# Preparing summed weight operands in two in-place series on SP's queue, with six own places for the sample states

## The chip, the cores and the metric

One core of one Trainium2 chip runs the whole program. The metric is device time in microseconds (us) of one execution. The engines are TensorE (PE, with its weight loads PEld), VectorE (DVE), ScalarE (ACT), GpSimd (POOL) and SyncE (SP). SP computes nothing here; it issues DMAs, in the order in which they stand in its stream, and where one has to wait, all behind it wait. The same holds for the DMAs that ACT issues between its own instructions.

## The reference

One inference step of two layers on a prompt of 2048 tokens and on 64 sample tokens (8 sequences of 8). Layer 0 is a gated DeltaNet, layer 1 a RetNet with 4 heads. The change lies in layer 1:

```
p = rmsnorm(x, norm_w) @ w_in           # x (L, 1024), w_in (1024, 6144)
q, k, v, gate = split(p)                # 4 heads: q,k 256 wide, v and gate 512 wide
q, k = rotary(q), rotary(k) / 16
o, S = retention(q, k, v, S0)           # S_t = gamma_h S_{t-1} + k_t^T v_t ; o_t = q_t S_t
o = rmsnorm(o, onorm) * silu(gate)
y = x + o @ w_out
```

The sample tokens start from given states (8 sequences x 4 heads x 256 x 512), which are read, used, updated and written back: 16 pieces of 128 x 512 in each head.

## The kernel before, in words

The prompt is cut into 4 blocks of 512 tokens (n = 0 to 3). Layer 0 runs over all blocks first, then layer 1; in both, four heads or groups follow one another in a block. Every matrix product in float32 is made of three products in a reduced format: each operand is split into a high part (a cast on ACT) and the rest (a subtraction on DVE). `wload` (L192) loads a weight tile into one of two places `wraw`, casts it on ACT (L196) and subtracts on DVE (L197).

Layer 1 computes the projections of block 0 in the plain way, with the 64 sample tokens beside them (width 576). Blocks 1 to 3 use a scheme with 7 products of half-size operands in place of 8 (`quad`, `vquad`, `seven`). It needs sums and differences of the quarters of each weight matrix, A21+A22 and so on, already split in two parts. They are prepared once, during block 0, and kept in DRAM (`wh_d`): 4 heads x 6 weight tiles x 4 combinations. That is the generator `prep_head` (L1022), four tasks in a chain. For each of the 24 weight tiles it loads two 128x1024 halves (`Rw`, tag "ta", 2 places), makes four sums of 128x512 on POOL (`Sm`, L1032 to L1035), splits each on ACT and DVE into `Wo` (tag "tc", 2 places), and stores it with 512 KB. All these loads and stores are issued by ACT.

The order comes from two levels. A small planner (`_Pipe`) advances a clock with each matmul it emits and lets side tasks (the retention `ret_prompt`, `ret_sample`, `prep_head`) emit their next piece when their time has come; a `yield 2.5` says that the next piece is due 2.5 us later by this clock. A tile scheduler then sets the final order of each engine's stream. Each engine runs its stream strictly in order.

At head 3 of block 0, `pipe.wait(ptask)` (L1524) emits all that is left of the preparation, and then `build_halves` (L1066) makes the halves of the activations for block 1. Its operands T2, T3 and N4 lie in the same places "ta", "tb" and "tc" that the preparation used. No projection of block 1 can start before.

`ret_sample` (L1226) runs once per head, for the 16 state pieces: a ring of five places, two in the tile "st" and three in the ring `xst`, which the output projection (`outproj_B`, L1322, tile `xr`) uses too. In groups of four pieces, PE multiplies the queries with the four states (`os`), then makes four updates (`ps`), DVE combines each with its state (L1303), SP stores it and loads the next piece into the place that came free (L1270).

Of the kernel before, what the change touches and what calls it, by code (L numbers as in the profile page):

```python
# [10 lines left out]
F32 = mybir.dt.float32  # L11
# [80 lines left out]
def tile_hybrid(ctx: ExitStack, tc: tile.TileContext, a: dict, S: int):  # L92
# [926 lines left out]
            return q[0][0], q[1][0], q[0][1], q[1][1]  # L1019
        return [src[j][:, 512 * i : 512 * i + 512] for j in range(2) for i in range(2)]  # L1020

    def prep_head(h):  # L1022
        pb = B.pb
        for t, (src, vkind) in enumerate(quads(h)):
            R = [pb.tile([128, 1024], F32, tag="ta", bufs=2, name="Rw") for _ in range(2)]
            for j in range(2):
                ACT.dma_start(R[j], src[j])
            A11, A12, A21, A22 = quarters(R, vkind)
            Sm = [pb.tile([128, 512], F32, tag="tb", bufs=4, name="Sm") for _ in range(4)]
            sm = [v3(x, 256) if vkind else x for x in Sm]  # L1030
            yield 5.0
            PL.tensor_tensor(sm[0], A21, A22, op=ALU.add)  # L1032
            PL.tensor_tensor(sm[1], sm[0], A11, op=ALU.subtract)
            PL.tensor_tensor(sm[2], A11, A21, op=ALU.subtract)
            PL.tensor_tensor(sm[3], A12, sm[1], op=ALU.subtract)  # L1035
            for i, x in enumerate(Sm):
                o = pb.tile([128, 2, 512], F32R, tag="tc", bufs=2, name="Wo")
                yield 1.5
                split(o[:, 0], o[:, 1], x)
                yield 2.5  # L1040
                ACT.dma_start(wh_d[h][4 * t + i], o.rearrange("p t c -> p (t c)").bitcast(F32))

    def wstream(h):

# [21 lines left out]
    def build_halves(n, rb):  # L1066
        pb = B.pb
        xs_, ts = [None] * 8, [None] * 8
        xn = [None] * 8
        for p in range(4):  # L1070
            xp = [sb.tile([128, 2, 2, XC], F32R, tag=f"xn{p}", name=f"xn{p}")]
            for j in range(2):
                xn[2 * p + j] = xp[0][:, j]
        T2, N4 = ([pb.tile([128, 2, 2, 256], F32R, tag=t, bufs=2, name=t) for _ in range(2)] for t in ("ta", "tc"))
        T3 = [pb.tile([128, 2, 256], F32R, tag="tb", bufs=4, name="tb") for _ in range(4)]
        T2, N4 = ([t[kt // 2][:, kt % 2] for kt in range(4)] for t in (T2, N4))
        l, r = slice(0, 256), slice(256, 512)
        for kt in range(4):
            xs, t = [], []
            for k in (kt, kt + 4):  # L1080
                x = xst("xs")
                nc.sync.dma_start(x[:, :TB], x1_d[k * 128 : (k + 1) * 128, n * TB : (n + 1) * TB])
                y = sb.tile([128, XC], F32, tag="tmp", bufs=2, name="xt")
                V.scalar_tensor_tensor(y[:, :TB], x[:, :TB], nw[:, 1, k : k + 1], rb[:, :TB],
                                       op0=ALU.mult, op1=ALU.mult)
                xs.append(x)
                t.append(y)
            lo_, hi_ = xn[kt], xn[kt + 4]
# [14 lines left out]

# [122 lines left out]
    def ret_sample(h, QRs, KRs, vraw, GTs, OG):  # L1226
# [16 lines left out]
        for half in range(2):  # L1243
            for k in range(2):
# [10 lines left out]
        ACT.activation(K3, v3(kT, 256), AF.Copy, scale=kd)  # L1255
        V.scalar_tensor_tensor(K3[64:128], v3(kT, 256)[64:128], kd[64:128], K3[64:128].bitcast(F32),
                               op0=ALU.mult, op1=ALU.subtract)
        loads, st2 = [], []

        def load(i):  # L1260
            if i >= 16:
                return
            if i % 5 < 2:
                if i % 5 == 0:
                    st2.append(pb.tile([128, 2, 512], F32, tag="st", name="st"))
                st = st2[-1][:, i % 5]
            else:
                st = xst("st")[:, :512]
            b, k = 4 * (i // 8) + i % 4, i // 4 % 2
            nc.sync.dma_start(st, a["state_ret"][b, h, k * 128 : (k + 1) * 128, :])  # L1270
            loads.append(st)

        for i in range(5):
            load(i)
        yield 6.0
        for half in range(2):
            o = po("os")
            mm(o, Ash[:, half * 128 : (half + 1) * 128], V3[:, half], start=True, stop=False)
            for k in range(2):
                yield LAT_ST  # L1280
                i0 = 8 * half + 4 * k
                t = pipe.t

                def query(b4):
                    r = slice(32 * b4, 32 * b4 + 32)
                    return mm(o[r], QRs[:, k, half * 128 + 32 * b4 : half * 128 + 32 * b4 + 32], loads[i0 + b4],
                              start=False, stop=(k == 1))

                last_in = query(3)
                with tc.issue_after(last_in.ins):  # L1290
                    for b4 in range(3):
                        query(b4)
                pipe.t = t + 1.0
                for b4 in range(4):
                    i = i0 + b4
                    st = loads[i]
                    Kt = pb.tile([128, 128], F32R, tag=("Kt", "Qc")[b4 % 2], name="Kts")
                    ACT.activation(Kt, K3[:, half, k * 128 : (k + 1) * 128].bitcast(F32), AF.Copy,
                                   scale=B.kms[:, h, b4 : b4 + 1])
                    yield 0.8  # L1300
                    p = pc("ps") if b4 % 2 == 0 else pf("ps")
                    mm(p, Kt, V3[:, half])
                    V.scalar_tensor_tensor(st, st, g8, p, op0=ALU.mult, op1=ALU.add)  # L1303
                    nc.sync.dma_start(a["ret_s"][4 * half + b4, h, k * 128 : (k + 1) * 128, :], st)
                    if i:
                        load(i + 4)
            yield from until(posts[-1])
            on = ret_on(o, h, 2)

# [97 lines left out]
    for n in range(NB):  # L1407
        for h in range(4):
# [66 lines left out]
            if start:  # L1475
# [1 line left out]
                pb = B.pb  # L1477
                Gs, GTs = GTs, pb.tile([128, 4, NS], F32, tag="GTs", bufs=2, name="GTs")
                V.tensor_copy(GTs, Gs)
                for j in range(BH):  # L1480
                    ptask = pipe.add(prep_head(j), 9, [ptask])
            if h == 3 and n + 1 < NB:
                rb = ret_rb(n + 1)
            pipe.wait(lastret)
# [36 lines left out]
                vraw = pb.tile([128, 512], F32, tag="p2", name="vraw")[:64]  # L1521
                ACT.copy(vraw, pvs[:64])
            if h == 3 and n + 1 < NB:
                pipe.wait(ptask)  # L1524
                xo = build_halves(n + 1, rb)
            end = n == NB - 1 and h == 3
            if pendB and not end:
# [141 lines left out]
```

## Time and profile before

| | us |
|---|---|
| median of 3 runs (3439.61 to 3457.56) | 3439.98 |
| the profiled execution | 3458.83 |
| its span | 3455.9 |
| layer 1, block 0, from the first prepared tile to the last value matmuls of head 3 | 1515 to 2027 |
| from there until the output projection of head 2 runs on | 2027 to 2085 |
| blocks 1 to 3 | 2100 to 3456 |

The profiled execution took 18.9 us longer than the median. PE is busy in 93% of the span. Rows say for an instruction when it starts, how long it takes, and in square brackets how long its engine had been idle and what ended that wait. TensorE's clock has two levels, 1.2 and 2.4 GHz; PEclk 0.92 means that the granted clock was on average 0.92 of the higher one.

### The profile page before, as it was taken

What the parts mean: (1) busy time and instruction counts of PE and PEld (TensorE: products, weight loads), DVE (VectorE), ACT (ScalarE), POOL (GpSimd) and SP (SyncE); (2) the same over time, 40 slices, a digit from 0 to 9 for tenths busy, and PEclk for the clock granted to TensorE, in tenths of its full rate; (3) what the DMA queues carried; (4) which work ended last, traced back from release to release, by engine and by line L of the source; (5) the groups of instructions that cost most, each with busy time, mean ns of one, the idle gap of its engine ahead of it and who ended that gap; (6) DMA issues with size and microseconds to landing.
All of it is one profiled execution on the core that took longest, in us unless ns stands there. A gap on an engine that the chain in (4) does not pass through costs nothing. (4 is left out here: it accounts for less than half of the span.)

```text
span 3455.9 us, 59249 instructions
## 1 busy us (share of the span) xinstructions
PE 3228.3 (93%) x21436; PEld 2820.6 (82%) x21436; DVE 2400.7 (69%) x5406; ACT 1582.9 (46%) x3655; POOL 494.5 (14%) x714
## 2 busy tenths in 40 slices
PE   7999999999999999998898868999999999999997
PEld 6999777778688788877777747889988899889896
DVE  6876888787868878556574666566676666776666
ACT  6555564455435555324242443344443344533443
POOL 1211011001010000012322230111101111111110
PEclk9999999999999999999999989999999999999999
DMA  4333544435443243456878777887677867778675
GB/s 131 96 95 100 176 126 132 132 102 157 120 138 109 88 135 83 142 190 229 293 250 289 246 247 230 271 276 252 228 253 251 279 242 244 235 270 286 216 246 171
DMA packets 371413, 669.79 MB, mean 194 GB/s; under 512 B 119456, under 2 KB 169392, under 8 KB 371120
## 3 DMA queue, kind: packets, MB, share of 16 engines
q1 hardware_dynamic: 350384, 590.49, 53.1%
q10 hardware_dynamic: 20736, 75.51, 6.0%
q8 instruction: 169, 2.77, 0.3%
q14 instruction: 124, 1.02, 0.1%
HBM read 517.08 MB, written 146.68 MB: 192 GB/s over the span
## 5 line engine op out<-in xcount | busy, mean ns | idle before, releaser
L101 PE MATMUL pp<-xn,w 128*128 128x288 f32 (+1 forms) x5456 | 1107.2, 351 | 21.8 <-DVE xr L1336 5.5
L101 PEld LDWEIGHTS pp<-xn,w 128*128 128x128 f32 x5456 | 861.6, 192 | 131.8 <-issue 18.5
L101 PE MATMUL pp<-OG,w 128*128 128x512 f32 (+1 forms) x2880 | 597.2, 366 | 27.4 <-DVE xr L1336 18.1
L101 PEld LDWEIGHTS pp<-OG,w 128*128 128x128 f32 x2880 | 491.8, 195 | 114.2 <-DVE xr L1336 18.0
L197 DVE TENSOR_TENSOR w<-wraw,w 128x1024 fp32r<-128x1024 f32 x272 | 347.4, 1278 | 97.3 <-ACT w L196 92.8
L196 ACT CAST w<-wraw 128x1024 fp32r<-128x1024 f32 x272 | 286.1, 1052 | 250.3 <-PE pp L101 126.8
L101 PE MATMUL sq<-xn,w 128*128 128x256 f32 x2304 | 310.6, 284 | 7.5 <-DVE GT L1106 3.5
L101 PEld LDWEIGHTS sq<-xn,w 128*128 128x128 f32 x2304 | 287.9, 188 | 15.1 <-issue 5.4
L210 ACT CAST w<-wraw 128x512 fp32r<-128x512 f32 x216 | 129.5, 623 | 218.5 <-PE pp L101 75.2
L1336 DVE TENSOR_TENSOR xr<-xr,pp 128x512 f32<-128x512 f32 (+1 forms) x160 | 92.4, 592 | 143.2 <-PE pp L101 105.9
L211 DVE TENSOR_TENSOR w<-wraw,w 128x512 fp32r<-128x512 f32 x216 | 147.9, 698 | 60.2 <-ACT w L210 56.7
L743 DVE SCALAR_TENSOR_TENSOR acc<-pp,cw,acc 128x511 f32<-128x511 f32 (+2 forms) x216 | 160.4, 743 | 20.6 <-ACT acc L740 20.2
L101 PE MATMUL sv<-w,xn 128*128 128x256 f32 x1152 | 147.1, 285 | 6.6 <-DMA w<-wh_d 5.1
L101 PEld LDWEIGHTS sv<-w,xn 128*128 128x128 f32 x1152 | 142.1, 192 | 8.9 <-DVE KR L1004 3.2
L101 PE MATMUL o<-Sc,Qc 128*128 128x512 f32 x360 | 100.9, 404 | 11.0 <-DVE Sc L211 5.9
L488 DVE TENSOR_TENSOR VP<-VP,tm 128x66 f32<-128x66 f32 (+26 forms) x510 | 107.0, 210 | 4.4
L486 DVE TENSOR_TENSOR tm<-LP,VP 128x66 f32<-128x66 f32 (+26 forms) x510 | 104.9, 206 | 6.1 <-DMA LP<-sl 2.1
L101 PE MATMUL p<-Vh,Kt 128*128 128x512 f32 x384 | 107.8, 412 | 0.0
L101 PE MATMUL pv<-w,xn 128*128 128x512 f32 x384 | 101.8, 413 | 4.0 <-ACT w L196 1.9
L210 ACT CAST Wo<-Sm 128x512 fp32r<-128x512 f32 x96 | 58.7, 617 | 96.1 <-DMA wh_d<-Wo 69.9
L210 ACT CAST OG<-og 128x256 fp32r<-128x256 f32 x192 | 71.6, 405 | 66.4 <-DVE og L1215 33.1
L1151 POOL TENSOR_TENSOR so<-oss,rsc 128x1 f32<-128x1 f32 x72 | 15.5, 215 | 580.8 <-ACT on L1149 580.8
(434 smaller groups left out, 5727.1 us busy)
## 6 DMA issues: line engine op xcount, KB each, us to landing
w<-wh_d SPq DMA_DIRECT2D x288, 512.0 KB, 5.4
wraw<-in_w_in_a SPq DMA_DIRECT2D x128, 512.0 KB, 3.7
wh_d<-Wo ACTq DMA_DIRECT2D x96, 512.0 KB, 4.6
x_d<-xr SPq DMA_DIRECT2D x160, 256.0 KB, 3.9
wraw<-in_w_qkg SPq DMA_DIRECT2D x144, 256.0 KB, 4.3
xr<-x_d SPq DMA_DIRECT2D x128, 256.0 KB, 4.5
wraw<-in_w_out_b SPq DMA_DIRECT2D x64, 512.0 KB, 4.2
wraw<-in_w_v SPq DMA_DIRECT2D x72, 256.0 KB, 5.1
```

Of the source, the lines that this page charges most:

```text
L101: ins = nc.tensor.matmul(out, lhsT, rhs, start=start, stop=stop)
L196: ACT.copy(w[:, 0, :], raw)
L197: V.tensor_tensor(w[:, 1, :], raw, w[:, 0, :].bitcast(F32), op=ALU.subtract)
L210: ACT.copy(hi, x)
L211: V.tensor_tensor(lo, x, hi.bitcast(F32), op=ALU.subtract)
L486: V.tensor_tensor(tv, LP[:, m, m + 1 : m + 1 + n].unsqueeze(2).to_broadcast([128, n, ncol]), VP[:, m, 0:ncol].unsqueeze(1).to_broadcast([1 ...
L488: V.tensor_tensor(VP[:, m + 1 : m + 1 + n, 0:ncol], VP[:, m + 1 : m + 1 + n, 0:ncol], tv, op=ALU.subtract)
L743: V.scalar_tensor_tensor(acc[:, sh:], ap[:, : TB - sh], cw[:, ct, j : j + 1], acc[:, sh:], op0=ALU.mult, op1=ALU.add)
L1151: PL.tensor_tensor(so, ss, B.rsc[:, h, col : col + 1], op=ALU.add)
L1336: V.tensor_tensor(xs[:, s:e], xs[:, s:e], p[:, : e - s], op=ALU.add)
```

## The change

The preparation becomes two tasks without a chain, `prep(0)` and `prep(1)`. Each handles one half (256 of 512 columns of every quarter, index `u`) of all 24 weight tiles. A step loads four quarters of 128x256 with four DMAs, makes the four sums with four POOL instructions of 128x256, casts all four in one ACT instruction of 128x1024 back into the tile that was loaded, subtracts in one DVE instruction in place in the sums, and stores the two parts with two DMAs of 512 KB in runs of 256 columns. The first series uses the two places of "ta", the second those of "tb" (now as large as "ta"). All six DMAs of a step are issued by SP. So each step needs both places of its series, and the next load goes into the place that the cast's result is stored from.

The 16 state pieces of a head use six places of their own ("st" with two, the freed "tc" with four) in heads 0 to 2; `xst` is then left to the output projection. Head 3, where "tc" holds N4, keeps five.

```
+    def halves_of(src, vkind, u):
+        if vkind:
+            return [src[j][:, 512 * u + 256 * i : 512 * u + 256 * i + 256] for i in range(2) for j in range(2)]
+        return [src[j][:, 512 * i + 256 * u : 512 * i + 256 * u + 256] for j in range(2) for i in range(2)]
...
-    def prep_head(h):
+    def prep(u):
         pb = B.pb
-        for t, (src, vkind) in enumerate(quads(h)):
-            R = [pb.tile([128, 1024], F32, tag="ta", bufs=2, name="Rw") for _ in range(2)]
-            for j in range(2):
-                ACT.dma_start(R[j], src[j])
-            A11, A12, A21, A22 = quarters(R, vkind)
-            Sm = [pb.tile([128, 512], F32, tag="tb", bufs=4, name="Sm") for _ in range(4)]
-            yield 5.0
-            PL.tensor_tensor(sm[0], A21, A22, op=ALU.add)
...
-            for i, x in enumerate(Sm):
-                o = pb.tile([128, 2, 512], F32R, tag="tc", bufs=2, name="Wo")
-                yield 1.5
-                split(o[:, 0], o[:, 1], x)
-                yield 2.5
-                ACT.dma_start(wh_d[h][4 * t + i], o.rearrange("p t c -> p (t c)").bitcast(F32))
+        tag = ("ta", "tb")[u]
+        for h, t in ((h, t) for h in range(BH) for t in range(6)):
+            src, vkind = quads(h)[t]
+            R = pb.tile([128, 4, 256], F32R, tag=tag, bufs=2, name="Rw")
+            Sm = pb.tile([128, 4, 256], F32, tag=tag, bufs=2, name="Sm")
+            A11, A12, A21, A22 = (R[:, i, :].bitcast(F32) for i in range(4))
+            for x, y in zip((A11, A12, A21, A22), halves_of(src, vkind, u)):
+                nc.sync.dma_start(x, y)
+            yield 6.0
+            PL.tensor_tensor(Sm[:, 0], A21, A22, op=ALU.add)
...
+            yield 4.5
+            ACT.copy(R, Sm)
+            V.tensor_tensor(Sm.bitcast(F32R), Sm, R.bitcast(F32), op=ALU.subtract)
+            yield 3.0
+            out = wh_d[h][4 * t : 4 * t + 4].rearrange("x p (l v c) -> p x l v c", l=2, v=2)[:, :, :, u, :]
+            nc.sync.dma_start(out[:, :, 0], R.bitcast(F32))
+            nc.sync.dma_start(out[:, :, 1], Sm)
+            yield 4.5
...
+        ring = 5 if h == 3 else 6
...
-            if i % 5 < 2:
-                if i % 5 == 0:
-                    st2.append(pb.tile([128, 2, 512], F32, tag="st", name="st"))
-                st = st2[-1][:, i % 5]
+            j = i % ring
+            if j < 2 or h < 3:
+                if j % 2 == 0:
+                    tag, bufs = ("st", 1) if j < 2 else ("tc", 2)
+                    st2[0] = pb.tile([128, 2, 512], F32, tag=tag, bufs=bufs, name="st")
+                st = st2[0][:, j % 2]
...
                     if i:
-                        load(i + 4)
+                        load(i + ring - 1)
...
-                for j in range(BH):
-                    ptask = pipe.add(prep_head(j), 9, [ptask])
+                ptask = [pipe.add(prep(u), 9, lat=9.0 * u) for u in range(2)]
...
-                pipe.wait(ptask)
+                pipe.wait(*ptask)
```

How the streams move is shown at three places. The numbers in the names tell buffers apart. The first is ACT's stream before, right behind the copies of head 3's values (`Vt`, `vraw`); `Wo<-Sm` is one cast of the preparation, `wh_d3` its place in DRAM.

```order
L210 CAST Wo_21820<-Sm_21812 128x512
L210 CAST Wo_21824<-Sm_21813 128x512
L1027 DMA Rw_21837<-in_w_v 128x1024
L1041 DMA wh_d3_76<-Wo_21820 128x1024
L1041 DMA wh_d3_76<-Wo_21824 128x1024
L196 CAST w_22072<-wraw_22071 128x1024
L210 CAST Wo_21828<-Sm_21814 128x512
L196 CAST w_22143<-wraw_22142 128x1024
L210 CAST Wo_21832<-Sm_21815 128x512
L1041 DMA wh_d3_76<-Wo_21828 128x1024
L1027 DMA Rw_21864<-in_w_v 128x1024
```

The changed stream, five short instructions behind the same copies; `Rw<-Sm` is one cast of a step, of twice the columns.

```order
L1045 CAST Rw_21737<-Sm_21738 128x1024
L1045 CAST Rw_21743<-Sm_21744 128x1024
L196 CAST w_21984<-wraw_21983 128x1024
L196 CAST w_22055<-wraw_22054 128x1024
L1045 CAST Rw_21765<-Sm_21766 128x1024
L1045 CAST Rw_21771<-Sm_21772 128x1024
L196 CAST w_22126<-wraw_22125 128x1024
L1045 CAST Rw_21793<-Sm_21794 128x1024
L210 CAST Sc_22408<-Sr_21521 128x512
L1045 CAST Rw_21799<-Sm_21800 128x1024
L1045 CAST Rw_21821<-Sm_21822 128x1024
L1045 CAST Rw_21827<-Sm_21828 128x1024
```

Before, 12 casts in all stand behind the last `Vt` copy, which is 3 of the 24 weight tiles, with ACT's own DMAs among them; now 10 casts (8 of them shown, 2 further on), which is 5 of the 24, and no DMA. The streams of the retention (`Sc`, and further on `Ah`) stand behind them.

SP's changed stream at the same place, for the last two steps of both series; `Rw<-in_w_v` are loads, `wh_d3<-Rw` and `wh_d3<-Sm` the stores of the two parts, the others tables.

```order
L1038 DMA Rw_21821<-in_w_v 128x256 x4
L1038 DMA Rw_21827<-in_w_v 128x256 x4
L1177 DMA rmk_22299<-in_rmask 128x128
L1473 DMA cs_22796<-in_rope 128x2x512
L1049 DMA wh_d3_76<-Rw_21821 128x4x256
L1050 DMA wh_d3_76<-Sm_21822 128x4x256
L1049 DMA wh_d3_76<-Rw_21827 128x4x256
L1050 DMA wh_d3_76<-Sm_21828 128x4x256
L1038 DMA Rw_21849<-in_w_v 128x256 x4
L1038 DMA Rw_21855<-in_w_v 128x256 x4
```

None of these loads and stores stood on SP before. The eight loads of a pair of steps stand behind all four stores of the pair before.

PE's stream before, at the states of the third head in block 0, from the last update `ps` of the third group of states to the queries `os` of the fourth; `pp<-xn` is projection work that fills the time.

```order
L101 MATMUL ps<-V_20757,Kts 128x512
L101 MATMUL pp<-xn_16129,w 128x288
L101 MATMUL pp<-xn_16144,w 128x288 x12
L101 MATMUL pp<-xn_16159,w 128x288 x12
L101 MATMUL pp<-xn_16114,w 128x288 x12
L101 MATMUL pp<-xn_16129,w 128x288 x12
L101 MATMUL pp<-xn_16144,w 128x288
L101 MATMUL os<-st,QRs 32x512 x4
```

The same place in the changed stream, from a little earlier.

```order
L101 MATMUL pp<-xn_16144,w 128x288 x3
L101 MATMUL ps<-V_20863,Kts 128x512
L101 MATMUL pp<-xn_16159,w 128x288 x4
L101 MATMUL ps<-V_20863,Kts 128x512
L101 MATMUL pp<-xn_16159,w 128x288 x8
L101 MATMUL os<-st,QRs 32x512 x4
```

The queries of the fourth group moved forward: 8 matmuls lie between the last update and them, where there were 50.

## Rows read from the trace of the kernel before

**Rows 1.** The head of the page.
```profile
span 3455.9 us, 59249 instructions
```

**Rows 2.** Stretches: us, busy us of each engine (instructions), PEclk, DMA share, GB/s.
```profile
1515.00:2027.00 512.00, 445.91 (x2521) 373.96 (x2520) 318.55 (x552) 203.66 (x423) 143.85 (x128) 0.92 0.76 263
2027.00:2085.00 58.00, 26.86 (x102) 18.19 (x101) 39.02 (x71) 26.87 (x57) 14.09 (x14) 0.67 0.55 192
...
2700.00:2800.00 100.00, 99.02 (x694) 91.74 (x693) 63.27 (x112) 39.67 (x82) 11.58 (x17) 1.00 0.74 251
```

**Rows 3.** Timeline of PE at the end of block 0: start, us, instruction, idle before.
```profile
2026.82 4.95 PE L101 MATMUL pp<-OG,w 128*128 128x288 f32 x36
...
2048.87 0.80 PE L101 MATMUL o<-Vh,Ah 128*128 128x512 f32 x1 [15.34 <-ACT Vh L210]
...
2085.14 5.17 PE L101 MATMUL pp<-OG,w 128*128 128x288 f32 x20 [1.67 <-DVE xr L1336]
```

**Rows 4.** Waits from 1515 to 2085 us: total, times, longest.
```profile
ACT Wo L210 <- DMA wh_d<-Wo: 69.9, 27, 5.3
...
PE os L101 <- DMA st<-in_state_ret: 31.0, 10, 6.9
...
DVE xr L1336 <- DMA xr<-x_d: 18.1, 8, 5.9
PE pp L101 <- DVE xr L1336: 17.0, 8, 5.5
...
ACT w L196 <- DMA xr<-x_d: 8.2, 1, 8.2
...
PE pv L101 <- ACT w L196: 1.9, 1, 1.9
```

**Rows 5.** The prepared operands `Wo` in the whole trace: ns min/median/max, first and last start.
```profile
L210 ACT CAST Wo<-Sm x96: 601/618/650, 1524.4 to 2065.6; 128x512 fp32r<-128x512 f32 x96
L211 DVE TENSOR_TENSOR Wo<-Sm,Wo x96: 675/686/1781, 1529.8 to 2066.3; 128x512 fp32r<-128x512 f32 x96
L1041 ACTq DMA_DIRECT2D wh_d<-Wo x96: 325/326/514, 1530.5 to 2067.1; - x96
```

**Rows 6.** The loaded tiles `Rw`: the sums made of them on POOL.
```profile
L1032 POOL TENSOR_TENSOR Sm<-Rw x24: 1259/1292/2092, 1521.0 to 2048.5; 128x512 f32<-128x512 f32 x24
```

**Rows 7.** The page's costliest groups: busy us, mean ns, idle before.
```profile
L197 DVE TENSOR_TENSOR w<-wraw,w 128x1024 fp32r<-128x1024 f32 x272 | 347.4, 1278 | 97.3 <-ACT w L196 92.8
L196 ACT CAST w<-wraw 128x1024 fp32r<-128x1024 f32 x272 | 286.1, 1052 | 250.3 <-PE pp L101 126.8
```

**Rows 8.** Groups of POOL by shape: sums of 128x256 in blocks 1 to 3.
```profile
L1106 POOL TENSOR_TENSOR GT<-GT 128x256 f32<-128x256 f32 x48 | 44.7, 931 | 146.6 <-DVE GT L1106 144.7
...
L1106 POOL TENSOR_TENSOR QR<-QR 128x256 f32<-128x256 f32 x24 | 17.9, 748 | 106.6 <-DVE QR L1106 105.7
```

**Rows 9.** DMA issues from 1515 to 2085 us: KB each, median us from issue to landing.
```profile
Rw<-in_w_qkg ACTq DMA_DIRECT2D x32, 512.0 KB, 5.0
st<-in_state_ret SPq DMA_DIRECT2D x48, 256.0 KB, 5.3
...
rms<-in_rms SPq DMA_DIRECT2D x3, 128.0 KB, 3.4
```

**Rows 10.** `Wo` from 2027 to 2085 us: its casts, and its stores' landing.
```profile
L210 ACT CAST Wo<-Sm x12: 614/618/622, 2027.5 to 2065.6; 128x512 fp32r<-128x512 f32 x12
...
DMA to landing us min/median/max: 2.6/3.2/6.8
```

**Rows 11.** Timeline of PE at sample states and output projection, block 0.
```profile
1724.19 3.73 PE L101 MATMUL pp<-xn,w 128*128 128x288 f32 x14 [5.55 <-DVE xr L1336]
...
1823.51 1.93 PE L101 MATMUL os<-st,QRs 128*32 128x512 f32 x8 [6.87 <-DMA st<-in_state_ret]
...
1979.48 6.81 PE L101 MATMUL pp<-xn,w 128*128 128x288 f32 x50
1990.07 1.94 PE L101 MATMUL os<-st,QRs 128*32 128x512 f32 x8 [3.79 <-DMA st<-in_state_ret]
```

**Rows 12.** Timeline of ACT before the gap at 1724 us.
```profile
1723.11 1.04 ACT L196 CAST w<-wraw 128x1024 fp32r<-128x1024 f32 x1 [8.20 <-DMA xr<-x_d]
```

**Rows 13.** Waits of SP's own queue from 1515 to 2085 us.
```profile
SPq L195 <- DVE w L197: 163.9, 35, 14.7
```

More of the change, by code (lines that the diff above doesn't have):

```diff
@@ L1020, in quarters @@
         return [src[j][:, 512 * i : 512 * i + 512] for j in range(2) for i in range(2)]
-    def prep_head(h):
-        pb = B.pb
-        for t, (src, vkind) in enumerate(quads(h)):
-            R = [pb.tile([128, 1024], F32, tag="ta", bufs=2, name="Rw") for _ in range(2)]
-            for j in range(2):
-                ACT.dma_start(R[j], src[j])
-            A11, A12, A21, A22 = quarters(R, vkind)
-            Sm = [pb.tile([128, 512], F32, tag="tb", bufs=4, name="Sm") for _ in range(4)]
-            sm = [v3(x, 256) if vkind else x for x in Sm]
-            yield 5.0
-            PL.tensor_tensor(sm[0], A21, A22, op=ALU.add)
-            PL.tensor_tensor(sm[1], sm[0], A11, op=ALU.subtract)
-            PL.tensor_tensor(sm[2], A11, A21, op=ALU.subtract)
-            PL.tensor_tensor(sm[3], A12, sm[1], op=ALU.subtract)
-            for i, x in enumerate(Sm):
-                o = pb.tile([128, 2, 512], F32R, tag="tc", bufs=2, name="Wo")
-                yield 1.5
-                split(o[:, 0], o[:, 1], x)
-                yield 2.5
-                ACT.dma_start(wh_d[h][4 * t + i], o.rearrange("p t c -> p (t c)").bitcast(F32))
+    def halves_of(src, vkind, u):
+        if vkind:
+            return [src[j][:, 512 * u + 256 * i : 512 * u + 256 * i + 256] for i in range(2) for j in range(2)]
+        return [src[j][:, 512 * i + 256 * u : 512 * i + 256 * u + 256] for j in range(2) for i in range(2)]
@@ new lines, in prep @@
+    def prep(u):
+        pb = B.pb
+        tag = ("ta", "tb")[u]
[8 more added lines that the diff above has]
+            PL.tensor_tensor(Sm[:, 0], A21, A22, op=ALU.add)
+            PL.tensor_tensor(Sm[:, 1], Sm[:, 0], A11, op=ALU.subtract)
+            PL.tensor_tensor(Sm[:, 2], A11, A21, op=ALU.subtract)
+            PL.tensor_tensor(Sm[:, 3], A12, Sm[:, 1], op=ALU.subtract)
+            yield 4.5
[6 more added lines that the diff above has]
+            yield 4.5
@@ L1073, in build_halves @@
                 xn[2 * p + j] = xp[0][:, j]
-        T2, N4 = ([pb.tile([128, 2, 2, 256], F32R, tag=t, bufs=2, name=t) for _ in range(2)] for t in ("ta", "tc"))
-        T3 = [pb.tile([128, 2, 256], F32R, tag="tb", bufs=4, name="tb") for _ in range(4)]
-        T2, N4 = ([t[kt // 2][:, kt % 2] for kt in range(4)] for t in (T2, N4))
+        T2, T3, N4 = ([pb.tile([128, 2, 2, 256], F32R, tag=t, bufs=2, name=t) for _ in range(2)]
+                      for t in ("ta", "tb", "tc"))
+        T2, T3, N4 = ([t[kt // 2][:, kt % 2] for kt in range(4)] for t in (T2, T3, N4))
         l, r = slice(0, 256), slice(256, 512)
@@ L1257, in ret_sample @@
                                op0=ALU.mult, op1=ALU.subtract)
-        loads, st2 = [], []
+        loads, st2 = [], [None]
+        ring = 5 if h == 3 else 6
         def load(i):
@@ L1271, in load @@
             loads.append(st)
-        for i in range(5):
+        for i in range(ring):
             load(i)
```

## The prediction

> **What bounds the kernel now.** I started at the head of the page [rows 1] and then asked for the busy times by stretch [rows 2]. They tell where the change can act at all. In blocks 1 to 3 PE works 99.02 of 100 us at clock 1.00; nothing of the preparation is left there. In block 0 of layer 1 (1515 to 2027 us, "stage A") PE works 445.91 of 512 us at a mean clock of 0.92, and in the 58 us behind it (the "tail") 26.86 us at 0.67. PE sets the pace, and what can be won or lost is PE's idle time and its lower clock in these 570 us.
>
> Next I read PE's timeline at the end of block 0 [rows 3]. The gap of 15.34 us ends with a copy of values on ACT, and PE is back at the output projection only at 2085.14. In between stand the last casts of the preparation, the halves for block 1 in the places that come free, and the retention behind those casts on ACT.
>
> Then the waits of this time [rows 4]. PE lost 31.0 us in 10 waits for sample states and 17.0 us in 8 waits for `xr`, the residual of the output projection. ACT waited 69.9 us for its own stores of `Wo`, and once 8.2 us in front of a weight cast for a load of another queue.
>
> **The change part by part.** The sum is made against the profiled execution, 3458.8 us; it is 18.9 us above the median, which is taken off at the end.
>
> *Casts, subtractions, sums.* Removed are 96 casts of 618 ns and 96 subtractions of 686 ns [rows 5], 59 and 66 us, and 96 POOL sums of about 1292 ns [rows 6]. Added are 48 casts of 128x1024, for which the weight cast of that shape has 1052 ns, and 48 subtractions at 1278 ns [rows 7]: 50 and 61 us. POOL gets 192 sums of half the columns; rows of 128x256 have 748 and 931 ns [rows 8], half of 1292 would be 0.65. Per tile POOL then needs 8 x 0.75 = 6.0 us against 4 x 1.29 = 5.2. ACT is busy 203.66 of 512 us and DVE 318.55, so in stage A all of this hides: 0. In the tail nothing covers it, and there it is counted below.
>
> *Issues.* ACT loses 144 issues of 326 ns, 47 us, and the 69.9 us of waits; both lie beside PE's work: 0 by themselves. SP gains 288, at the same price 94 us.
>
> *Tail.* Before, 12 quarter casts (3 tiles) stand behind the last value copy, the last starting at 2065.6, 38 us behind the first [rows 10]. Now it is 10 half casts, 5 tiles, in pairs, since SP has the loads of both series behind all four stores. The first pair is through about 6 us after the value copy (two casts, one subtraction, and 2.6 us of ACT's other work in front, an estimate). Then a pair of steps takes:
> - one store issue 0.33 and four load issues 4 x 0.33 = 1.3;
> - the landing of a 128x256 load: 3.4, the row of the same 128 KB [rows 9];
> - eight sums on POOL, 8 x 0.748 = 6.0 (the two series meet there);
> - the last cast and subtraction, 1.05 + 1.28.
>
> That is 13.4 us, the landing of the stores hidden beneath the other series; four pairs make 53.6. Before, the last cast began 38.8 us behind 2026.82, and PE resumed 19.5 us later (2085.14 - 2065.6). Now the end of the last subtraction comes at 6 + 53.6; its last cast started 2.3 earlier, at 57.3. T2 and T3 need the places that the last stores empty, which adds an issue and a landing, 0.33 + 3.2: 57.3 + 19.5 + 3.5 = 80.3 against 58.3, so **+22 us**. Bounds: with 0.65 for a sum and 2.6 for a landing a pair takes 12, which gives +16; with 0.931 for a sum and the landing of 5.0 that ACT's loads have [rows 9] it is 16.5, +34; with 6.8, the longest landing of the tail [rows 10], and sums at 0.931 it is 18.3, +42; loads held back behind a store that takes that long give 20, +48. ACT's work behind the casts is in the 19.5 already.
>
> *Sample states.* PE's rows [rows 11] show two such gaps, 6.87 and 3.79 us. In the second, 6.81 us of projection work (50 matmuls, 0.136 each) did not cover the state's way, which was 10.6 us (1990.07 - 1979.48). A sixth place lets the last load of a group go out one update earlier. But the new order puts the queries forward: 8 matmuls in front of them, 1.1 us of cover, where there were 50; the displaced work isn't lost, only the cover. Most: -31, all of it; least: +10, where 5.7 us of cover is lost at two places and a little returns. I take -8, about a quarter of the waits, since one update's spacing is small against 10.6.
>
> *`xr`.* The 18.1 us that DVE waited in front of these additions end on the load of `xr` [rows 4], which SP issues when its queue comes to it and a place is free. For a gain: the states of heads 0 to 2 leave the three places of `xst` to the projection, and ACT's and SP's DMAs no longer stand in each other's way. The row of 8.20 us [rows 12] shows what that did: a weight cast on ACT stood behind a load of `xr` for which it has no use, and PE's gap of 5.55 us on `xr` followed at 1724.19 [rows 11]. Against it: 288 issues and their waits now share SP's queue with these loads. Bounds -17.0 and +10, an estimate: two more gaps like that one. I take -6, the one gap that has a visible cause on ACT.
>
> *Clock.* The mean of 0.92 in stage A, with 0.5 and 1.0 as its levels, means 16% of 512, 82 us, at the lower level. At that level half the speed is lost, at most 41 us, where PE has work in all of it; 82 - 66 = 16 us at the lower level, a loss of 8, would be the least, if all 66 us of idle time lay at that level. With 14 of the 66 idle us gone, a fifth, I take a fifth of 41, -8; bounds 0 and -25.
>
> *SP.* Its own queue already waited 163.9 us for places of weight tiles in stage A [rows 13], and PE hardly waited for a weight then: its own waits on a cast `w` come to 1.9 us [rows 4]. 94 us of issues and the new waits (a store behind its subtraction, a load behind a landing) are queued in front of weight loads, state loads and state stores. I take 0, as PE did not feel these waits so far; bounds 0 and +20, an eighth of the 163.9 us turned into gaps of PE.
>
> The Trainium skill, "DMA: Bandwidth & Descriptors", section "Issuing engines are not separate DMA queues", speaks against the gain: all DMAs run on the same 16 engines, so starting them on several engines saves only the time of starting. By that rule the terms of `xr`, states and clock would be 0, which is the mechanism of rival 3. The trace doesn't agree in full: ACT's 69.9 us of waits in front of its own next work are more than the 47 us of issue time.
>
> Sum: -8 - 6 - 8 + 0 + 22 = 0. So 3458.8 us in the profile's terms stay, and with 18.9 off a median of **3440 us**: what stage A gains, the tail takes.
>
> **The rivals.**
>
> *1. Faster: ACT's release carries.* With ACT free and states early, half the state waits (-15), all of `xr` (-17) and the whole bound of the clock (-25) go: -57. With the shortest tails (+16 to +22) the net is near -38: 3440 - 38 = 3402. For it: the 27 waits of ACT [rows 4] and the mean clock of 0.67 to 0.92 [rows 2], which falls with each gap. Against it: the order that moves the queries forward, and ACT's low load.
>
> *2. Slower: the lock-step at the end.* No step of a series can load before it has stored, and SP ties the two series to each other. If a pair takes 20 us the tail is +48, and with stage A at -18 the net is +30: 3470. It decides from a pair of about 17.5 us on (four pairs of 4.1 more, +38, net +17 at the gain of 22 taken above). For it: the landing of 6.8 us in this very place, SP's longer queue, and 4 pairs in a row with nothing beneath. Against it: the median landing of 3.2 [rows 10].
>
> *3. The change doesn't do what it says.* Six places are used up by the earlier queries, and the moved issues free only time that was hidden: stage A 0, tail +22, 3440 + 22 = 3462. For it: the 1.1 us of cover, and PE's 31.0 us that hang on a way of 10.6 us which no place shortens. Against it: the row of 8.20 us.
>
> **How the numbers follow.** What a measurement of this kernel can tell from no change is about 0.5%, 17 us: faster is below 3423, slower above 3457. Forecast 0.36 (its own range 3420 to 3458; 0.34 of it within 0.5%, 0.02 faster), rival 1 0.30 (3385 to 3423), rival 2 0.25 (3458 to 3490), rival 3 0.09 (0.06 slower, 0.03 within). This gives faster 0.32, within 0.37, slower 0.31. Rivals 1 and 2 lie on both sides, so the range reaches into both: from 3399, which leaves 0.10 below, to 3475, which leaves 0.10 above.
>
> **What would show it.** In the changed profile: a time from the last value copy to PE's return of about 80 us, in which pairs of casts follow one another every 13.4 us (12 or less speaks for rival 1, 17.5 or more for rival 2); waits of PE for states near 23 us and for `xr` near 11 in block 0; a mean clock there above 0.92; no waits of ACT for the preparation's stores; SP's waits in front of weight loads without a gap of PE behind them. The forecast is wrong if the casts of the last pairs don't wait for their loads at all (then the tail's term falls), or if PE's gaps in stage A end on weights.

## The result and the profile after

| | before | changed |
|---|---|---|
| median of 12 runs each, us | 3445.03 | 3469.81 |
| ratio, 95% interval | | 1.0063 [1.0045, 1.0081] |
| profiled execution, us | 3458.83, a second one 3452.41 | 3472.95 |
| its span | 3455.9, 3450.3 | 3471.0 |

The change made the kernel 0.6% slower (the ratio is estimated from all runs; the quotient of the two medians is 1.0072). The time lies inside the range on record and 30 us above its likeliest value. Four times of a profile tell most of what follows: **F**, the start of the first batch of output projection behind head 3's values (36 matmuls); **C**, the start of the preparation's last cast; **R**, PE's return to the output projection; and the span's end.

| | F | C | R | R - C | end - R |
|---|---|---|---|---|---|
| before | 2026.8 | 2065.6 | 2085.1 | 19.5 | 1370.8 |
| before, second trace | 2021.3 | 2058.4 | 2077.8 | 19.4 | 1372.5 |
| changed | 2018.1 | 2078.2 | 2099.6 | 21.4 | 1371.4 |

All of the difference arises before R. In the changed kernel F comes earlier, by 8.7 us against the first trace of before and by 3.2 against the second, but C and R come later. The busy times of the changed kernel by stretch, cut at F (engines in the order PE, PEld, DVE, ACT, POOL; then PEclk, DMA share, GB/s), answer to [rows 2]:

```profile
1515.00:2018.00 503.00, 438.37 (x2535) 369.90 (x2533) 311.41 (x511) 199.52 (x384) 160.95 (x200) 0.94 0.78 254
2018.00:2100.00 82.00, 25.34 (x95) 19.27 (x96) 42.02 (x73) 27.48 (x53) 29.50 (x38) 0.62 0.68 219
```

Against the first trace of before, stage A (up to F) became 8.7 us shorter and the tail (F to R) 23.2 us longer. PE's timeline in the tail, against [rows 3]:

```profile
2018.14 7.58 PE L101 MATMUL pp<-OG,w 128*128 128x288 f32 x36 [5.62 <-ACT w L196]
2059.12 1.22 PE L101 MATMUL ap<-QR,KR 128*128 128x128 f32 x4 [33.41 <-DVE A L1193]
...
2099.64 1.57 PE L101 MATMUL pp<-OG,w 128*128 128x288 f32 x5 [14.94 <-DVE xr L1349]
```

Two gaps, 33.41 and 14.94 us, make the tail. The first ends on a masked product `A` of the retention, which stands on DVE behind a subtraction of the preparation. The second is the time in which DVE makes the halves of the activations for block 1 (2084.84 to 2098.80), behind which the addition to `xr` stands; their loads stand on SP behind the last stores of the preparation. ACT's timeline shows what the subtraction waits for, the casts of the last pairs:

```profile
2030.64 1.04 ACT L1045 CAST Rw<-Sm 128x1024 fp32r<-128x1024 f32 x1 [2.78 <-POOL Sm L1043]
...
2041.23 1.04 ACT L1045 CAST Rw<-Sm 128x1024 fp32r<-128x1024 f32 x1 [8.61 <-POOL Sm L1043]
...
2045.40 1.04 ACT L1045 CAST Rw<-Sm 128x1024 fp32r<-128x1024 f32 x1 [2.60 <-POOL Sm L1043]
2056.45 1.04 ACT L1045 CAST Rw<-Sm 128x1024 fp32r<-128x1024 f32 x1 [10.01 <-POOL Sm L1043]
2060.28 1.04 ACT L1045 CAST Rw<-Sm 128x1024 fp32r<-128x1024 f32 x1 [2.79 <-POOL Sm L1043]
```

The second casts of the pairs lie 14.8 and 14.9 us apart, and each first cast has waited 8 to 10 us for its sums. SP's timeline of one such pair:

```profile
2042.31 0.38 SPq L1049 DMA_DIRECT2D wh_d<-Rw  x1
2043.68 0.38 SPq L1050 DMA_DIRECT2D wh_d<-Sm  x1
2046.47 0.36 SPq L1049 DMA_DIRECT2D wh_d<-Rw  x1
2047.72 0.36 SPq L1050 DMA_DIRECT2D wh_d<-Sm  x1
2048.13 4.63 SPq L1038 DMA_DIRECT2D Rw<-in_w_v  x8
```

The first store of the first series was issued at 2042.31, but its next loads had to stand until 2048.13, behind the second store of the other series. Then the waits of block 0, to be read beside [rows 4] (total, times, longest):

```profile
ACT Rw L1045 <- POOL Sm L1043: 120.3, 36, 10.0
...
PE ap L101 <- DVE A L1193: 33.4, 1, 33.4
...
PE pp L101 <- ACT w L196: 18.9, 4, 6.0
...
PE os L101 <- DMA st<-in_state_ret: 10.0, 4, 5.7
```

PE's waits for states fell from 31.0 to 10.0 us. In their place stand waits for weights, which hardly existed before. ACT hardly waits for the preparation's stores any more (4.5 us in one piece, 69.9 before), but 120.3 us for the sums in front of its casts. SP's own waits, beside [rows 13]:

```profile
SPq L1049 <- ACT Rw L1045: 62.6, 23, 5.0
...
SPq L195 <- DVE w L197: 22.4, 10, 5.4
SPq L1050 <- DVE Sm L1046: 19.7, 19, 2.0
```

SP now stands at least 82 us in front of the preparation's stores. Its wait for places of weight tiles fell from 163.9 to 22.4 us: it used to be early with the weights, and is so no longer. Before, 38 of the 51 weight loads of this time were issued within 0.3 us of a DVE subtraction that freed a place, and one came more than 8 us behind it; in the changed kernel it is 11 of 50, and 17 came more than 8 us behind. PE's four waits for weights (18.9 us) are of this kind: both places had been free for 25.6, 9.5, 25.0 and 18.9 us when their loads were issued. By their landing times, the weights then stood about 1 to 2.5 us more on ACT, behind a cast of the preparation that waited for its sums, as in front of PE's wait of 6.04 us at 1964.58:

```profile
1962.54 1.04 ACT L1045 CAST Rw<-Sm 128x1024 fp32r<-128x1024 f32 x1 [8.14 <-POOL Sm L1043]
1963.49 1.04 ACT L196 CAST w<-wraw 128x1024 fp32r<-128x1024 f32 x1
```

### The profile page after: what moved, and what is told of

Read it like the earlier page. It is cut to its first block, busy times and chain, and to the rows that moved or that the text cites. A ratio compares the mean times of both kernels' runs of the same rounds, so it can differ in the third digit from the quotient of the medians.

```text
span 3471.0 us, 59507 instructions
## 1 busy us (share of the span) xinstructions
PE 3214.7 (93%) x21436; PEld 2812.2 (81%) x21436; DVE 2393.1 (69%) x5358; ACT 1578.0 (45%) x3607; POOL 527.7 (15%) x810
## 4 chain that ended last, share of the span: by engine, by line
PE 58%; DVE 12%; DMA 12%; ACT 6%; POOL 4%; issue 4%; SPq 2%; POOLq 0%; DVEq 0%; ACTq 0%
PE pp L101 32%; PE sq L101 7%; PE o L101 4%; DMA w<-wh_d 3%; PE sv L101 3%; PE p L101 3%; PE kyd L101 2%; PE oT L110 1%; DVE w L197 1%; DMA wraw<-in_w_v 1%; SPq L1038 1%; DMA wraw<-in_w_qkg 1%; POOL so L587 1%; POOL Sm L1041 1%; ACT w L196 1%
## 5 line engine op out<-in xcount | busy, mean ns | idle before, releaser
L1046 DVE TENSOR_TENSOR Sm<-Sm,Rw 128x1024 fp32r<-128x1024 f32 x48 | 61.3, 1278 | 85.6 <-ACT Rw L1045 48.1
L1045 ACT CAST Rw<-Sm 128x1024 fp32r<-128x1024 f32 x48 | 50.2, 1049 | 128.5 <-POOL Sm L1043 120.3
```

What stands on the lines that cost most here:

```text
L1045: ACT.copy(R, Sm)
L1046: V.tensor_tensor(Sm.bitcast(F32R), Sm, R.bitcast(F32), op=ALU.subtract)
```

## The experiments

Each ratio is to the kernel before in the same session (its medians there were 3444.7 to 3448.8), with its 95% interval.

**e1: the old ring of five places, in the changed kernel.**

```
-        ring = 5 if h == 3 else 6
+        ring = 5
-            if j < 2 or h < 3:
+            if j < 2:
```

> The changed kernel with one part undone: the sample states keep the old ring of five places (two in 'st', three in xst, shared with the output projection). Preparation as in the change. Theory A (the two parts act apart: the ring and the free xst took PE's waits for states from 31.0 to 10.0 us and for xr in block 0 from 17.0 to 3.2, and the preparation made the loss): PE's waits for states and xr in block 0 come back to 40 us or more together, the time is 3485 to 3500. Rival B (the waits shrank because loads and stores land faster now, 3.6 us for xr in place of 5.3, 4.5 for states in place of 5.3; the places do nothing): 3465 to 3475, state waits below 18 us. Tail the same in both: about 80 us, pairs of casts 14.7 us apart.

Measured 3481.2, 1.0093 [1.0071, 1.0115]. The time lies between the two forecasts, in neither. Theory A's mechanism is refuted: PE's waits for states were 1.2 us and for `xr` 2.3 in block 0, fewer than with six places, which agrees with rival B. The tail was 81.9 us, as both had it. The last cast came at 2095.6, 17 us later than in the changed kernel (this profiled execution lies 10.7 us above the median of its kernel, that of the change 3.1). So the places did not remove these waits. e12 takes this up.

**e2: earlier due times of the steps.**

```
-            yield 6.0 ... yield 4.5 ... yield 3.0 ... yield 4.5
+            yield 4.5 ... yield 3.0 ... yield 2.0 ... yield 3.5
```

> The changed kernel with the planner's due times of a preparation step cut from 18 to 13 us (4.5, 3.0, 2.0, 3.5). Same instructions; in ACT's stream 2 casts instead of 10 stand behind the last value copy of head 3. Theory A (the loss is the 23 us by which the tail grew, made by four dependent pairs of steps with nothing beneath): the tail falls from 81 to 45 to 60 us, the time to 3440 to 3452. Rival C (the loss is SP's and the DMAs' load in block 0, wherever the steps stand: denser steps make the weights later, which was 18.9 us of PE's waits): the tail falls, but the waits for weights in stage A rise by as much, 3460 to 3475.

Measured 3474.6, 1.0079 [1.0061, 1.0097]. Rival C holds by its time. F to R fell from 81.5 to 34 us, as theory A wanted, but only because F moved back by 52 us, to 2070.7. The last cast came at 2080.2, as before the edit (2078.2). Some of PE's waits in block 0 show a part of what held F up:

```profile
PE pp L101 <- ACT w L196: 22.3, 7, 5.6
...
PE os L101 <- DMA st<-in_state_ret: 14.4, 5, 4.7
...
PE pv L101 <- ACT w L196: 9.0, 2, 7.0
```

The waits for weights rose from 21.2 to 31.3 us, which is 10 of the 52 and not as much as the tail lost; where the rest of the delay comes from is open. ACT's order shows the way of these waits: casts of the preparation that are put earlier in its stream and still come no earlier in time stand in front of weight casts.

**e3: all six DMAs of a step on ACT.**

```
-            nc.sync.dma_start(x, y)                # 4 loads; the 2 stores likewise
+            ACT.dma_start(x, y)
```

> The changed kernel with all six DMAs of a preparation step issued by ACT, as before the change. In ACT's stream 6 casts stand behind the last value copy. Theory A: SP is free of the stores that wait for a subtraction, so PE's waits for weights fall from 18.9 to under 6 us; with two pairs fewer in the tail (2 x 14.7 = 29 us) the time is 3425 to 3445. Rival D (an issue that has to wait costs the same on either engine; on ACT it holds up the casts of weights and of the retention, which PE needs too): waits of PE on ACT's results rise instead, 3450 to 3475.

Measured 3478.1, 1.0082 [1.0063, 1.0101]. Theory A fails; rival D's mechanism holds, though its time is passed by 3 us. PE waited 28.8 us for states, with six places, and 31.2 us in one piece for a weight cast that stood on ACT behind the preparation.

**e4: two loads of 256 KB in place of four.**

```
-            for x, y in zip((A11, A12, A21, A22), halves_of(src, vkind, u)):
-                nc.sync.dma_start(x, y)
+            for x in range(2): ...  nc.sync.dma_start(Rf[:, 2 * x : 2 * x + 2], y)
```

> The changed kernel with the four 128x256 loads of a step joined to two of 256 KB: 96 issues fewer on SP. Casts behind the last value copy: 10 as in the change. Theory A (eight load issues of 4.66 us stand in each pair's chain of 14.7 us): a pair takes 12 to 13 us, the tail 72 to 76, the time 3460 to 3466, a little less if the weights come earlier too. Rival E (the transfer sets the time, not its issue, and two loads land later than four small ones): pair 14 to 15.5, 3466 to 3474.

Measured 3467.8, 1.0050 [1.0031, 1.0068], against 1.0063 [1.0045, 1.0081]: no difference that can be told. In the tail the pairs were still 14.5 us apart and more (2022.4, 2037.1, 2055.9). The number of issues is not what limits a pair, as rival E said. This run shows more: PE's waits for states and weights were down to 2.9 and 4.4 us, F came at 1999.2, 19 us earlier than in the changed kernel, and R still only 3 us earlier (2096.7). The tail took up the rest, 97.5 us.

**e5: the kernel before with its preparation's loads and stores on SP.**

```
-                ACT.dma_start(R[j], src[j])
+                nc.sync.dma_start(R[j], src[j])
-                ACT.dma_start(wh_d[h][4 * t + i], ...)
+                nc.sync.dma_start(wh_d[h][4 * t + i], ...)
```

> The kernel before with one thing changed: the loads and stores of its preparation are issued by SP in place of ACT. Theory F (formed on the runs so far: PE's waits for states and xr come from ACT and SP issuing side by side, not from the number of places; and block 0 ends some 20 us behind the last cast of the preparation): both waits together fall from 48 to under 20 us; but in ACT's stream 28 quarter casts (7 tiles) stand behind the last value copy, where there were 12, so the tail grows by about 4 x 12.7 us less what it overlaps: 3470 to 3500. Rival G (the six places removed the waits): they stay above 40 us here, and the time is 3490 or more.

Measured 3482.6, 1.0100 [1.0075, 1.0125]. This is the queue move with the old tiles and the old ring, and by the medians it costs more than the whole change (the intervals overlap). The waits of PE up to 2085 us are those of theory F:

```profile
PE pp L101 <- DVE xr L1336: 6.5, 4, 2.4
...
PE os L101 <- DMA st<-in_state_ret: 4.4, 5, 1.1
```

That is 10.9 us where there were 48, and F came 32 us earlier (1994.5). And yet PE then stood 78.7 us in a tail of 112 us, 54 longer than before, with 7 tiles behind the last value copy: theory F's price was about 4 x 12.7. SP stood 103.2 us in front of the stores (for a subtraction on DVE), and the next loads behind them. Weights are not the reason here: 42.5 of the 163.9 us in front of their loads were left, and PE waited 1.9 us for them.

**e6: half of the preparation.** Heads 2 and 3 are not prepared and use the operands of heads 0 and 1; the results that hang on them are therefore not the reference's.

```
-        for h, t in ((h, t) for h in range(BH) for t in range(6)):
+        for h, t in ((h, t) for h in range(2) for t in range(6)):
-                    nc.sync.dma_start(o.bitcast(F32), wh_d[h][4 * t + x - 4])
+                    nc.sync.dma_start(o.bitcast(F32), wh_d[h % 2][4 * t + x - 4])
```

> The changed kernel with half of its preparation left out: the operands of heads 2 and 3 are not prepared, those of heads 0 and 1 are read in their place. From the middle of stage A on there is no preparation. Theory F (preparation and projections hold each other up in the same streams all through block 0): PE's waits between 1800 us and the last value copy fall from 30 us or more to under 12, PE returns within 50 us of the last value copy, and the time is 3385 to 3410. Rival H (in stage A PE waits for the states and the weights of its own, and only the tail belongs to the preparation): the tail alone falls, 30 to 35 us: 3432 to 3442.

Measured 3369.0, 0.9781 [0.9754, 0.9808], below the range of theory F and nearer to it than to rival H. By stretch; the preparation's last cast starts at 1809.0, so the second has almost none:

```profile
1515.00:1790.00 275.00, 244.56 (x1451) 206.44 (x1449) 171.40 (x282) 116.44 (x229) 86.96 (x111) 0.96 0.77 254
1790.00:1970.00 180.00, 176.25 (x1032) 150.75 (x1033) 109.09 (x211) 66.19 (x136) 12.98 (x21) 0.97 0.58 190
```

Almost without the preparation PE is busy 176 of 180 us, F comes at 1970.1 and R 12.3 us behind it. In the changed kernel the same part took 228 us (1790 to 2018) and the tail 81.5. So half of the preparation costs some 100 us of block 0, though ACT is busy 40% of stage A, POOL 32% and DVE 62%. The edit also takes its transfers away (DMA share 0.58, where the changed kernel has 0.79 from 1790 to 2018 us); what they cost and what the order of the streams costs is not told apart.

**e7: stores on ACT, loads on SP.**

```
-            nc.sync.dma_start(out[:, :, 0], R.bitcast(F32))
-            nc.sync.dma_start(out[:, :, 1], Sm)
+            ACT.dma_start(out[:, :, 0], R.bitcast(F32))
+            ACT.dma_start(out[:, :, 1], Sm)
```

> The changed kernel with the two stores of a step issued by ACT, the loads by SP as in the change. One cast stands behind the last value copy in ACT's stream. Theory F: the waits for states and xr come back, to 25 to 48 us, as ACT issues again; the preparation's last cast moves little, since its steps wait in ACT's stream for PE's work instead, and so the time stays at 3455 to 3480. Rival A (what stands behind the last value copy makes the loss): tail below 55 us, time 3435 to 3450.

Measured 3449.3, 1.0004 [0.9987, 1.0022]: the whole loss is gone. It is nearer to rival A than to theory F, whose figure failed: the last cast did move, from 2078.2 to 2044.9, and PE returned at 2069.6, 18.1 us behind an F that itself came 33 us later (2051.5). The waits for states and `xr` were 18.0 and 13.8 us, as F said. SP didn't wait less than in the changed kernel, but now in front of loads, until the stores had emptied the tile that they go into:

```profile
SPq L1038 <- DMA wh_d<-Rw: 96.5, 27, 8.5
SPq L195 <- DVE w L197: 56.5, 21, 12.7
```

So how long SP stands does not decide by itself. With e2 beside it, A is refined: the order must put the preparation earlier, and the preparation must be able to follow.

**e8: the kernel before, unchanged.**

> The kernel before once more, unchanged, for a second trace of it: its first profiled execution lay 13.8 us above the median. Theory: the difference lies in block 0 (1515 to 2085 us), where waits decide, and blocks 1 to 3 take 1371 us again; the return of PE behind the tail then comes near 2071. Rival: the difference is spread over the span as clock.

It took 3452.4. R came at 2077.8, 7.4 us earlier than in the first trace (the forecast of 2071 was too bold), and what follows took 1372.5, 1.7 longer. So these two executions of one kernel differ in block 0, where waits decide, and little behind it.

**e9: loads on ACT, stores on SP** (e7 with the two groups exchanged).

> The changed kernel with the four loads of a step issued by ACT, the stores by SP as in the change; the mirror of the run with the stores on ACT (3449). Four casts stand behind the last value copy. Theory L (on SP's queue the loads of both series stand behind all four stores of a pair, and a store waits for a subtraction; it is this lock-step that makes the preparation end late, and taking either group off the queue undoes it): the last cast comes at 2045 to 2062, PE returns at 2068 to 2085, time 3445 to 3462. Rival J (the stores that wait on SP do the harm by themselves, to weights and states behind them): the time stays at 3464 to 3480, with weight waits of PE over 15 us.

Measured 3458.4, 1.0039 [1.0024, 1.0054]; last cast 2060.3, R 2085.0. All three lie in the ranges of theory L (the trace is of the fastest of six executions, 3451.1). Against the changed kernel's 1.0063 the intervals overlap, so by the time alone this run doesn't settle it; PE's waits for weights do, 2.2 us where rival J wanted over 15.

**e10: e7 with the two loads of e4.** No further edit.

> The changed kernel with the stores of a step on ACT and its four loads joined to two of 256 KB, on SP. No cast stands behind the last value copy, 13 of 48 behind head 2's. Theory L: the preparation ends before 2035, PE returns by 2060, time 3425 to 3444. Rival K (what is placed earlier in the streams only makes PE's weights and states later, as with the cut due times at 3475): PE's waits in stage A rise by 15 us or more, time 3447 to 3470.

Measured 3438.9, 0.9980 [0.9963, 0.9997], as theory L said. The last cast came at 2007.4, before F (2029.4), and the tail was 13 us. Here the preparation no longer ends last. (This profiled execution lies 17.8 us below the median of its kernel, so its trace flatters it.)

**e11: the kernel before with its loads on SP, the stores left on ACT** (the first of the two edits of e5).

> The kernel before with the loads of its preparation (two of 512 KB in a tile) issued by SP, the stores by ACT as before. No cast of the preparation stands behind the last value copy, where there were 12. Theory L (loads that do not stand behind stores let the preparation run ahead, whatever its tiles): tail below 50 us, PE's waits for states and xr fall a little, time 3415 to 3438. Rival K (what is placed earlier only delays PE's own work): 3440 to 3465.

Measured 3427.7, 0.9951 [0.9934, 0.9969], as theory L said: the lowest median of all that do the whole work, faster than both kernels (its interval just touches e10's). PE's timeline at the end of block 0:

```profile
2031.85 4.96 PE L101 MATMUL pp<-OG,w 128*128 128x288 f32 x36
...
2050.29 9.92 PE L101 MATMUL pp<-OG,w 128*128 128x288 f32 x57 [2.04 <-DVE xr L1336]
```

F is 5 us later than in [rows 3], but R comes 35 us earlier: 18.4 us of tail in place of 58.3. SP kept its lead with the weights:

```profile
SPq L195 <- DVE w L197: 121.4, 34, 15.5
```

**e12: e10 with the old ring** (the edit of e1).

> The run with stores on ACT and two loads (3439), with the sample states back in the old ring of five places: what the six places are worth once the preparation no longer ends last. Theory M (the places are worth nothing by themselves; the 11 us that the old ring cost with all DMAs on SP came from the later end of the preparation): 3430 to 3445. Rival N (the six places are worth some 10 us of PE's waits): 3447 to 3456, with PE's waits for states above 35 us, where there were 26.0.

Measured 3446.0, 0.9993 [0.9980, 1.0006]; it misses both forecasts by 1 us. PE's waits for states were 25.3 us, where e10 had 26.0, so rival N's mechanism does not hold; the last cast came 38 us later (2045.7) than in e10's trace. The intervals of e10 and e12 overlap: a small worth of the places, by way of the order and not by the states' waits, stays open.

**Taken together.** Ratios to the kernel before, by the engine that issues the preparation's loads and stores:

| loads, stores on | tiles of before | tiles of the change |
|---|---|---|
| ACT, ACT | 1 | 1.0082 |
| SP, SP | 1.0100 | 1.0063 |
| SP, ACT | 0.9951 | 1.0004 |
| ACT, SP | not run | 1.0039 |

In both columns, loads and stores on one queue are slower than loads on SP and stores on ACT, by intervals that don't touch. On one queue, a load stands behind stores that wait for a subtraction; with loads and stores on two queues it doesn't. Which way round matters too: e9 is slower than e7 by intervals that don't touch. In each of these edits the scheduler also ordered the streams anew; a change of queue with the order held fixed was not tried, so the share of each stays open.

## Why the prediction was right or wrong

**The tail: right in its mechanism, and in its size partly by luck.** Forecast 80.3 us from F to R, measured 81.5; forecast growth 22, measured 23.2 against [rows 3] (25.0 against the second trace). A pair was to take 13.4 and took 14.5 to 14.9, the last 18.0, so four took 62.1 where 53.6 was forecast. In the pair from 2045.40 to 2060.28 the way from the first load issue to the first sum took 5.3 us (4.7 counted) and the eight sums 6.8 (6.0 counted); the eight issues that stand in a row (4.63 us, where four of 0.33 were counted) lie mostly beneath the landing, which fits e4. In the last pair POOL also stood for the retention. Against that, the first pair was through 0.3 us behind F, where 6 was forecast, and PE came back 21.4 us behind the last cast, where the prediction had an issue, a landing and 19.5, that is 23. These errors cancel.

**Stage A: wrong.** Forecast 22 us shorter, measured 8.7 (F from 2026.8 to 2018.1; 3.2 against the second trace). The prediction's terms there:
- *Sample states*, -8: the waits fell by 21.0. The reason given, a sixth place, was wrong too. The waits go by the queue of the stores: with the stores on SP they were 10.0, 1.2, 14.4, 2.9, 4.4, 6.9 and 4.7 us (changed, e1, e2, e4, e5, e6, e9), with the stores on ACT 31.0, 27.5, 28.8, 18.0, 26.0, 21.8 and 25.3 (before, e8, e3, e7, e10, e11, e12), with five or six places alike. What passes from the one queue to the other was not measured.
- *`xr`*, -6: in stage A the waits fell from 17.0 to 3.2 (18.1 less the 14.94 of the tail), that is -13.8. Right in sign, at twice the size.
- *Clock*, -8: PE's busy time fell from 445.9 to 438.4 at 0.94 in place of 0.92, which is -7.5. The size is right, but not by the way that was given: the idle time that was to shrink by 14 us hardly did, and against the second trace (443.2 busy) it is -4.8.
- *SP*, 0: **this is the step that failed.** "I take 0, as PE did not feel these waits so far": the 163.9 us in front of weight loads were read as a wait that costs nothing. They were the lead that SP had. With the preparation's 288 DMAs on SP, 22.4 us of it were left, and PE waited 18.9 us for weights in stage A. That is the prediction's own sign of being wrong ("if PE's gaps in stage A end on weights"), and nearly the whole bound of +20. The lead that is left goes by how many DMAs of the preparation SP has: none, 163.9 and 153.6 us (before, e8; 123.2 in e3); 48, 121.4 (e11); 96, 41.1 to 82.8 (e9, e10, e12); 144, 42.5 (e5); 192, 38.1 and 56.5 (e4, e7); 288, 17.3 to 22.4 (changed, e1, e2). Only with 288 did PE wait more than 9 us for weights (21.2, 16.9 and 31.3 with those of the values), e3 aside, where their casts stood on ACT. In all PE's idle time in stage A went from 66.1 to 64.6 us (63.1 in the second trace of before): of the 34.8 us of waits that went, 33.3 came back as others, 18.9 of them for weights, 5.6 in one piece for the retention's keys on ACT, and the rest in small ones that no run explains.

**The sum.** Its form failed too: it adds a tail of fixed length to what stage A gains. In e4 stage A was 27.6 us shorter than in the first trace of before, more than the 22 of the forecast, and R came at 2096.7 all the same, since the preparation's last cast came only 3 us earlier (2075.1). So the SP term explains why F came too late for the forecast, not why the kernel lost: that is the late end of the preparation, which e7, e10 and e11 undo. By the numbers: 0 by the forecast, +14.1 between the two profiled executions (23.2 - 8.7 = 14.5 at R). The rest of the 24.8 us between the medians is in the reference: the first trace of before lies 13.8 us above its median, that of the changed kernel 3.1. A forecast that works with one trace carries that.

**The rivals.** Rival 2's time (3470) is the measured one, but not by its price: a pair took 14.7 and not 20 us. It is the forecast's tail with a smaller gain in stage A, so the agreement is in part luck. Its place and mechanism, the lock-step on SP, are what e5, e7 and e11 point to. Rival 3 came near with 3462 but had the mechanism wrong, since the waits that it kept did go. Rival 1 rested on ACT's release: ACT's 69.9 us became 120.3 us of another wait.

The Trainium skill's rule that the prediction weighed ("DMA: Bandwidth & Descriptors", "Issuing engines are not separate DMA queues") is about transfers, and no run here speaks against it there. But the same transfers, issued by other engines, gave 3482.6, 3446.2 and 3427.7 us (e5, before in e5's session, e11): in these kernels, whose order moved with the queue, it counted which waiting issue stands in front of which.

## What to carry to other kernels

A long wait for a free place, on a queue that nobody waits for, is not free slack: it is how far that queue runs ahead, new work on it is paid from there, and it costs once little is left (22 us here, not yet at 38). Don't put stores that wait for a result on the queue whose loads feed the next step: one queue for each was worth 1.5% here, with the order that came with it (e11 against e5). When waits go and the time doesn't fall, look for what ends last: here PE returned 18 to 28 us behind the preparation's last cast wherever that cast came behind or close to the last projections, and moving that cast earlier in the stream (e2) helped nothing until the preparation could follow (e7, e10, e11).

## What the runs showed of the hardware that was not expected

A POOL sum of 128x256 takes 0.72 us, but 1.59 while DVE subtracts 128x1024:

```profile
2041.84 0.73 POOL L1040 TENSOR_TENSOR Sm<-Rw 128x256 f32<-128x256 f32 x1
...
2042.31 1.34 DVE L1046 TENSOR_TENSOR Sm<-Sm,Rw 128x1024 fp32r<-128x1024 f32 x1 [7.64 <-DMA Sr<-sr_d]
2042.65 1.59 POOL L1041 TENSOR_TENSOR Sm<-Sm,Rw 128x256 f32<-128x256 f32 x1
```

This recurs in each pair, since the two series meet there, and is 0.9 of its 14.7 us. Of the 192 sums 23 took over 1.5 us, and each of them lay beside a subtraction of 128x1024 for at least 1 us; in the pairs of the tail they end 0.6 us behind its end. And a load issue of 128x256 on SP takes 0.58 us on average in a run of eight (4.63), not the 0.33 of the shortest.
